# Six five-product pairs of an up projection: the work on their left forms put in program order on TensorE, ScalarE, GpSimd and VectorE

## The chip, the cores and the metric

The kernel runs on one core of one Trainium2 chip. The metric is the device time of one execution in microseconds; the core has TensorE (PE, with its weight loads PEld), VectorE (DVE), ScalarE (ACT), GpSimd (POOL) and SyncE (SP), which work side by side, each in its own order, and wait for one another on semaphores.

## The reference

One layer of a decoder over 1024 positions of width 1024: three token mixers, cross-attention, and a gated MLP. The change lies in the first matrix product of the MLP, `h @ w_up`:

```python
def conv_gated_ffn(h, w_up, conv_w, conv_b, w_down):
    u, v = jnp.split(h @ w_up, 2, axis=-1)
    u = lax.conv_general_dilated(u, conv_w[:, None, :], window_strides=(1,),
                                 padding=[(CONV_W - 1, 0)],
                                 dimension_numbers=('NWC', 'WIO', 'NWC'),
                                 feature_group_count=D_FF) + conv_b
    return (jax.nn.silu(u) * v) @ w_down
```

D_FF is 2816, so `w_up` has 5632 columns: 22 blocks of 128 for `u` and 22 for `v`.

## The kernel before, in words

**Pairs and products.** `ffn_up` goes through 22 pairs. A pair is block f of `u` and block f of `v`; their weights are the 2 x 2 blocks A11, A12, A21, A22 of a left matrix (512 rows of the contraction each), and the activations are the 2 x 2 blocks of the right one. A scheme of Strassen's kind computes the pair with seven block products in place of eight. The right forms (B11, B21, T1 to T4, B22) are made once, ahead of the loop. The left forms (A11, A12, A22 and the sums S1 to S4) are made for each pair by the generator `left` (L1292). For the first six pairs (`ne` = 6) two products, with A11 and A12, are computed earlier by `ahead` and kept in DRAM (`part`), so that these pairs have five: T2 with S2, T3 with S3, T1 with S1, T4 with A22, B22 with S4, in this order in the program. The sixteen others have seven.

**A left form.** Three steps: GpSimd makes the sum (L1308; A22 needs none), ScalarE rounds it to the high half (the cast, L1315), and the rest becomes the low half by a subtraction (L1316), on VectorE and GpSimd in turn from form to form. The form's tile `wf` has four buffers, two of each of the tags `whi` and `wlo`; a new form takes its buffer when the product that read the old one has ended.

**A product.** `prod` (L1319 to L1325): 12 matmuls of 128 x 128 by 128 x 512, that is four steps of the contraction by three combinations of halves (high-high, high-low, low-high).

**Where the products go.** T2 writes `ps_b`, one bank of PSUM. T3, T1, T4 and B22 share one tile `ps_cd` of two banks: T3 and then T4 write its first half c, T1 and then B22 its second half d. Two such tiles alternate from pair to pair. Between them VectorE reads: u2 after T2 (L1384), u3 after T3 (L1386), the upper half of vt after T1 (L1388), the lower half of vt after T4 (L1393), u after B22 (L1395). Then ScalarE's y (L1397), two y steps of VectorE (L1398, L1399), Silu on ScalarE (L1400), y times vt on VectorE (L1401); in even pairs a difference within y (L1404), in odd pairs three sums over the two pairs (L1414 to L1416, one on VectorE and two on GpSimd); DMAs of SyncE write y and the sums to DRAM, and load the next raw weights (`load`, six buffers: three pairs).

**What sets the order.** Nothing in this code writes the order out by hand. The kernel is traced in program order, and the scheduler of the framework then places each engine's instructions by priority and by when it takes their inputs to be ready, so that products of neighbouring pairs stand between one another.

Of the kernel before, what the change touches and what calls it, by code (L numbers as in the profile page):

```python
# [12 lines left out]
F32 = mybir.dt.float32  # L13
# [4 lines left out]
ALU = mybir.AluOpType  # L18
# [78 lines left out]
class K:  # L97
# [1197 lines left out]
    def left(self, r1, r2, which, sp):  # L1295

        nc = self.nc
        V, A, G = nc.vector, nc.scalar, nc.gpsimd
        q = {f"A{n}{k + 1}": r[:, 4 * k:4 * k + 4, :] for n, r in ((1, r1), (2, r2)) if r is not None for k in range(2)}
        sums = {"S1": ("A21", "A22", ALU.add), "S2": ("S1", "A11", ALU.subtract), "S3": ("A11", "A21", ALU.subtract),  # L1300
                "S4": ("A12", "S2", ALU.subtract)}

        def get(n):
            if n not in q:
                a, b, op = sums[n]
                a, b = get(a), get(b)
                q[n] = sp.tile([P, 4, P], F32, tag=n, name=n, bufs=2 if n in ("S1", "S2") else 1)
                G.tensor_tensor(out=q[n], in0=a, in1=b, op=op)  # L1308
            return q[n]

        for n in which:
            x = get(n)
            self.nform = getattr(self, "nform", 0) + 1
            f = self.wp.tile([P, 2, 4, P], F32R, tag=("whi", "wlo")[self.nform % 2], name="wf")
            A.copy(out=f[:, 0], in_=x)  # L1315
            (V if self.nform % 2 else G).tensor_tensor(out=f[:, 1], in0=x, in1=f[:, 0].bitcast(F32), op=ALU.subtract)  # L1316
            yield f

    def prod(self, ps, f, x, start, stop):  # L1319
        n = 0  # L1320
        for k in range(4):
            for a, b in ((0, 0), (0, 1), (1, 0)):
                self.nc.tensor.matmul(ps, lhsT=f[:, a, k, :], rhs=x[b][:, k, :], start=(start and n == 0), stop=(stop and n == 11),  # L1323
                                      skip_group_check=not start)
                n += 1  # L1325

    def ffn_up(self, X, act, sums, part, spill):

# [2 lines left out]
        V, A, G, T = nc.vector, nc.scalar, nc.gpsimd, nc.tensor  # L1331
        with tc.tile_pool(name="up", bufs=1) as sp:
# [4 lines left out]
            ne = part.shape[1]  # L1337

            def load(m, bufs=6):
                n = next(nraw) % bufs  # L1340
                r = self.wp.tile([P, NK, P], F32, tag="raw", name="raw") if n < 2 else \
                    self.res.tile([P, NK, P], F32, tag=f"r{n + 6 - bufs}", name="raw")
                nc.sync.dma_start(out=r, in_=I["t_up"][m])
                return r
# [84 lines left out]
            rs = [load(0), load(NFF)]  # L1429
            for f in range(NFF):  # L1430
                nx = [load(f + 1), load(NFF + f + 1)] if f + 1 < NFF else None
                pair(f, rs)
                rs = nx

# [217 lines left out]
```

## Time and profile before

| | |
|---|---|
| time, median of 3 runs | 2406.57 us (2404.03 to 2408.04) |
| the profiled execution | 2406.16 us, its span 2404.4 us |
| TensorE busy | 2308.2 us, 96% of the span |
| VectorE, ScalarE, GpSimd busy | 57%, 38%, 28% |
| mean granted clock of TensorE | 0.989 |
| first product of the five-product pairs | 1773.47 us after the span's start |

The stretch of the six pairs runs from 1773 to some 1880 us of the span; seven-product pairs follow, and from about 2170 us on the down projection, `ffn_down`. In the rows further down, times are microseconds from the start of the span; a row of the timeline gives an instruction's start, its duration, engine, source line, operation, output <- inputs, and in brackets the engine's idle time before it and what ended that. Matmuls are pipelined: in an unbroken row they follow each other by 0.23 us though each shows 0.39. "PEclk" is the granted clock as a share of the full 2.4 GHz; 0.5 is the lower level of 1.2 GHz.

### The profile page before, as it was taken

To read this page: it belongs to the slowest core of one execution; us is meant where nothing else is said; L and a number is where in the kernel's file an instruction comes from. 1 tells how busy PE (TensorE), PEld (TensorE's weight loads), DVE (VectorE), ACT (ScalarE), POOL (GpSimd) and SP (SyncE) were. 2 spreads that over 40 slices of the span, in tenths; PEclk is the share of its full clock that TensorE was granted. 3 is DMA by queue.
4 is the path that set the end of the run, shared out by engine and by line. 5 is a ranking of instruction groups with operands and counts; after the bars stand their busy time and mean duration, and the time that the engine had idled before them with its cause. 6 is when DMAs were issued, how large, how long until landed. Compare 5 with 4: busy or idle time off the path is not lost. (4 is left out here: it accounts for less than half of the span.)

```text
span 2404.4 us, 34900 instructions
## 1 busy us (share of the span) xinstructions
PE 2308.2 (96%) x13988; PEld 1883.5 (78%) x13988; DVE 1364.3 (57%) x2114; ACT 908.5 (38%) x1430; POOL 670.6 (28%) x564
## 2 busy tenths in 40 slices
PE   7999999899999999999999999999888999999998
PEld 7887768686778787887878787888766788888886
DVE  6446375747334647545464454544636666667776
ACT  6542213131223535444353223343333334335443
POOL 1011011110101333214223350142346665652001
PEclk9999999999999999999999999999999999999999
DMA  8653322221212111111103663223354232228633
GB/s 305 220 177 119 96 62 93 62 82 48 85 45 99 53 45 44 45 53 44 53 27 99 221 205 123 88 88 126 111 168 139 101 113 93 106 73 280 218 96 122
DMA packets 110930, 266.14 MB, mean 111 GB/s; under 512 B 27248, under 2 KB 31984, under 8 KB 110768
## 3 DMA queue, kind: packets, MB, share of 16 engines
q1 hardware_dynamic: 108656, 258.25, 32.2%
q0 software_dynamic: 1248, 4.46, 0.5%
q8 instruction: 110, 1.80, 0.3%
q10 hardware_dynamic: 864, 1.20, 0.1%
q14 instruction: 52, 0.43, 0.1%
HBM read 194.40 MB, written 69.47 MB: 110 GB/s over the span
## 5 line engine op out<-in xcount | busy, mean ns | idle before, releaser
L155 PE MATMUL ps_d<-hThi,whi 128*128 128x512 f32 x1056 | 426.7, 404 | 2.6 <-DVE Ktt L261 2.2
L157 PE MATMUL ps_d<-hTlo,whi 128*128 128x512 f32 x1056 | 424.9, 403 | 0.0
L159 PE MATMUL ps_d<-hThi,wlo 128*128 128x512 f32 x1056 | 424.3, 402 | 0.0
L140 ACT CAST whi<-raw 128x1024 fp32r<-128x1024 f32 (+1 forms) x170 | 166.9, 988 | 329.1 <-PE ps_d L157 153.5
L155 PEld LDWEIGHTS ps_d<-hThi,whi 128*128 128x128 f32 x1056 | 200.2, 190 | 45.5 <-issue 3.2
L143 DVE TENSOR_TENSOR wlo<-raw,whi 128x1024 fp32r<-128x1024 f32 (+1 forms) x125 | 157.6, 1268 | 137.4 <-ACT whi L140 137.4
L157 PEld LDWEIGHTS ps_d<-hTlo,whi 128*128 128x128 f32 x1056 | 200.3, 190 | 43.0 <-issue 4.6
L159 PEld LDWEIGHTS ps_d<-hThi,wlo 128*128 128x128 f32 x1056 | 200.1, 190 | 43.1 <-issue 4.2
L143 POOL TENSOR_TENSOR wlo<-raw,whi 128x1024 fp32r<-128x1024 f32 (+1 forms) x45 | 96.3, 2141 | 436.0 <-ACT whi L140 389.1
L1508 PE MATMUL ps_dn<-wd,ap 128*128 128x512 f32 x924 | 210.2, 389 | 0.0
L1508 PEld LDWEIGHTS ps_dn<-wd,ap 128*128 128x128 f32 x924 | 173.3, 188 | 36.4 <-DVE wd L1475 0.4
L1315 ACT CAST wf<-S 128x512 fp32r<-128x512 f32 x88 | 54.6, 622 | 163.3 <-PE ps_cd L1323 73.7
L1113 POOL TENSOR_SCALAR ms<-ms 128x1 f32<-128x1 f32 x30 | 11.4, 381 | 345.0 <-ACT fin L1112 159.7
L1474 ACT CAST ap<-acr 128x512 fp32r<-128x512 f32 x77 | 47.9, 622 | 105.1 <-PE ps_dn L1508 59.6
L745 DVE CUSTOM_DVE_ANT_0 a_p<-ps_s,a_bias 128x512 f32<-128x512 f32 (+3 forms) x96 | 51.7, 552 | 52.0 <-PE ps_s L743 46.8
L1316 POOL TENSOR_TENSOR wf<-S,wf 128x512 fp32r<-128x512 f32 x44 | 63.1, 1435 | 55.3 <-ACT wf L1315 55.3
L755 ACT ACTIVATE a_p<-a_p,a_nm 128x128 f32<-128x128 f32 (+7 forms) x64 | 49.1, 769 | 77.2 <-POOL a_nm L751 59.7
L159 PE MATMUL ps_d<-ohi,wlo 128*128 128x512 f32 x192 | 75.2, 392 | 2.0 <-DVE wlo L143 2.0
L1475 DVE TENSOR_TENSOR ap<-acr,ap 128x512 fp32r<-128x512 f32 x77 | 54.0, 701 | 39.7 <-ACT ap L1474 39.7
L155 PE MATMUL ps_d<-ohi,whi 128*128 128x512 f32 x192 | 75.2, 392 | 0.0
L157 PE MATMUL ps_d<-olo,whi 128*128 128x512 f32 x192 | 75.1, 391 | 0.0
L1308 POOL TENSOR_TENSOR S<-raw 128x512 f32<-128x512 f32 x44 | 58.9, 1341 | 36.7 <-DVE wf L1316 21.8
(435 smaller groups left out, 5354.6 us busy)
## 6 DMA issues: line engine op xcount, KB each, us to landing
raw<-t_in SPq DMA_DIRECT2D x66, 512.0 KB, 3.6
raw<-t_up SPq DMA_DIRECT2D x50, 512.0 KB, 3.5
th_dram<-th SPq DMA_DIRECT2D x24, 512.0 KB, 2.8
mth<-th_dram SPq DMA_DIRECT2D x24, 512.0 KB, 3.7
wdr<-ffn_w_down SPq DMA_DIRECT2D x44, 256.0 KB, 4.4
acr<-act_dram SPq DMA_DIRECT2D x44, 256.0 KB, 3.5
act_dram<-y SPq DMA_DIRECT2D x20, 512.0 KB, 2.6
acr<-sums_dram SPq DMA_DIRECT2D x33, 256.0 KB, 2.6
```

The lines of the kernel that those rows point to most:

```text
L140: nc.scalar.copy(out=hi, in_=raw)
L143: eng.tensor_tensor(out=lo, in0=raw, in1=hi.bitcast(F32), op=ALU.subtract)
L155: nc.tensor.matmul(o, lhsT=hi[:, k, :], rhs=xhi(k, h), start=(k == 0), stop=False)
L157: nc.tensor.matmul(o, lhsT=hi[:, k, :], rhs=xlo(k, h), start=False, stop=False)
L159: nc.tensor.matmul(o, lhsT=lo[:, k, :], rhs=xhi(k, h), start=False, stop=(k == nk - 1))
L745: V.tensor_tensor_reduce(out=p_[:, a:b], in0=ps[:, 0:b - a], in1=bias[:, 1024 - n + a:1024 - n + b], op0=ALU.add, op1=ALU.max, scale=1.0, ...
L755: A.activation(out=pr[c][:, 0:n], in_=pr[c][:, 0:n], func=AF.Exp, bias=nm[:, c:c + 1], accum_out=Z[:, c:c + 1])
L1308: G.tensor_tensor(out=q[n], in0=a, in1=b, op=op)
L1315: A.copy(out=f[:, 0], in_=x)
L1316: (V if self.nform % 2 else G).tensor_tensor(out=f[:, 1], in0=x, in1=f[:, 0].bitcast(F32), op=ALU.subtract)
L1475: behind("V", lambda: V.tensor_tensor(out=t[:, 1], in0=z, in1=t[:, 0].bitcast(F32), op=ALU.subtract))
L1508: T.matmul(ps[t], lhsT=a[:, p, P * t:P * t + P], rhs=w[:, q, :], start=(not onto and j == 0 and n == 0), stop=(j == NJ - 1 and n == 2), sk ...
```

## The change

A helper `inorder` and a dictionary `kinds` are added. While `kinds` is a dictionary (from pair 0 until pair 6 begins), each call chains its instruction behind the last one of the same kind, by `issue_after`, an ordering edge without a semaphore. The kinds are "T" (matmuls of a product, chained by the product's last matmul), "A" (casts on ScalarE), 0 (sums and subtractions on GpSimd) and 1 (subtractions on VectorE). VectorE's reads of PSUM, the y steps, Silu and the DMAs are not chained. Computations and their number are the same in both kernels: 11670 matmul instructions, 2116 of VectorE, 1304 of ScalarE, 569 of GpSimd, 657 of SyncE. The order differs in one stretch of each engine (487 of TensorE's positions, 82 of VectorE's, 61 of ScalarE's, 64 of GpSimd's, 43 of SyncE's).

```diff
--- before.py
+++ after.py
@@ -1305,24 +1305,36 @@
                 a, b, op = sums[n]
                 a, b = get(a), get(b)
                 q[n] = sp.tile([P, 4, P], F32, tag=n, name=n, bufs=2 if n in ("S1", "S2") else 1)
-                G.tensor_tensor(out=q[n], in0=a, in1=b, op=op)
+                self.inorder(0, lambda: G.tensor_tensor(out=q[n], in0=a, in1=b, op=op))
             return q[n]
 
         for n in which:
             x = get(n)
             self.nform = getattr(self, "nform", 0) + 1
             f = self.wp.tile([P, 2, 4, P], F32R, tag=("whi", "wlo")[self.nform % 2], name="wf")
-            A.copy(out=f[:, 0], in_=x)
-            (V if self.nform % 2 else G).tensor_tensor(out=f[:, 1], in0=x, in1=f[:, 0].bitcast(F32), op=ALU.subtract)
+            e = self.nform % 2
+            self.inorder("A", lambda: A.copy(out=f[:, 0], in_=x))
+            self.inorder(e, lambda: (G, V)[e].tensor_tensor(out=f[:, 1], in0=x, in1=f[:, 0].bitcast(F32), op=ALU.subtract))
             yield f
 
+    kinds = None
+
+    def inorder(self, n, f):
+        if self.kinds is None:
+            return f()
+        with self.tc.issue_after(self.kinds[n].ins) if n in self.kinds else ExitStack():
+            self.kinds[n] = f()
+
     def prod(self, ps, f, x, start, stop):
-        n = 0
-        for k in range(4):
-            for a, b in ((0, 0), (0, 1), (1, 0)):
-                self.nc.tensor.matmul(ps, lhsT=f[:, a, k, :], rhs=x[b][:, k, :], start=(start and n == 0), stop=(stop and n == 11),
-                                      skip_group_check=not start)
-                n += 1
+        def run():
+            n = 0
+            for k in range(4):
+                for a, b in ((0, 0), (0, 1), (1, 0)):
+                    i = self.nc.tensor.matmul(ps, lhsT=f[:, a, k, :], rhs=x[b][:, k, :], start=(start and n == 0),
+                                              stop=(stop and n == 11), skip_group_check=not start)
+                    n += 1
+            return i
+        self.inorder("T", run)
 
     def ffn_up(self, X, act, sums, part, spill):
 
@@ -1429,6 +1441,8 @@
             rs = [load(0), load(NFF)]
             for f in range(NFF):
                 nx = [load(f + 1), load(NFF + f + 1)] if f + 1 < NFF else None
+                if f in (0, ne):
+                    self.kinds = None if f else {}
                 pair(f, rs)
                 rs = nx
```

On TensorE, in the first pair, after T1 (`ps_cd_14614` belongs to the first pair, `ps_b2_14721` and `ps_cd_14722` to the second). Before:

```order
L1323 MATMUL ps_cd_14614<-T1lo_14151,wf_14655 128x512
L1323 MATMUL ps_cd_14614<-T1hi_14150,wf_14655 128x512
L1323 MATMUL ps_b2_14721<-T2hi_14141,wf_14729 128x512
L1323 MATMUL ps_b2_14721<-T2lo_14142,wf_14729 128x512
L1323 MATMUL ps_cd_14722<-T3hi_14291,wf_14747 128x512
L1323 MATMUL ps_cd_14722<-T3lo_14292,wf_14747 128x512
L1323 MATMUL ps_cd_14614<-T4hi_14159,wf_14671 128x512
```

After:

```order
L1333 MATMUL ps_cd_14614<-T1lo_14151,wf_14655 128x512
L1333 MATMUL ps_cd_14614<-T1hi_14150,wf_14655 128x512
L1333 MATMUL ps_cd_14614<-T4hi_14159,wf_14671 128x512
L1333 MATMUL ps_cd_14614<-T4lo_14160,wf_14671 128x512
L1333 MATMUL ps_cd_14614<-T4hi_14159,wf_14671 128x512 x2
```

The matmuls of the second pair's T2 and T3 that stood between T1 and T4 now stand behind B22 of the first pair.

On VectorE, from the first pair's u to the second pair's lower vt (`u2_14723`, `u3_14724`, `vt_14720` belong to the second pair, `y_14705` to the first). Before:

```order
L1384 TENSOR_TENSOR u2_14723<-ps_b2_14721,s1_14717 128x512
L1386 TENSOR_TENSOR u3_14724<-ps_cd_14722,u2_14723 128x512
L1398 SCALAR_TENSOR_TENSOR y_14705<-u_14365,par_70,y_14705 128x1024
L1399 SCALAR_TENSOR_TENSOR y_14705<-u_14365,par_70,y_14705 128x1024
L1316 TENSOR_TENSOR wf_14879<-S1_14841,wf_14879 128x512
L1388 TENSOR_TENSOR vt_14720<-ps_cd_14722,u3_14724 128x512
L1401 TENSOR_TENSOR y_14705<-y_14705,vt_14612 128x1024
L1404 TENSOR_TENSOR y_14705<-y_14705 128x512
L1393 TENSOR_TENSOR vt_14720<-ps_cd_14722,u2_14723 128x512
```

After:

```order
L1410 SCALAR_TENSOR_TENSOR y_14705<-u_14365,par_70,y_14705 128x1024
L1396 TENSOR_TENSOR u2_14723<-ps_b2_14721,s1_14717 128x512
L1411 SCALAR_TENSOR_TENSOR y_14705<-u_14365,par_70,y_14705 128x1024
L1398 TENSOR_TENSOR u3_14724<-ps_cd_14722,u2_14723 128x512
L1413 TENSOR_TENSOR y_14705<-y_14705,vt_14612 128x1024
L1416 TENSOR_TENSOR y_14705<-y_14705 128x512
L1317 TENSOR_TENSOR wf_14845<-S2_14843,wf_14845 128x512
L1400 TENSOR_TENSOR vt_14720<-ps_cd_14722,u3_14724 128x512
L1405 TENSOR_TENSOR vt_14720<-ps_cd_14722,u2_14723 128x512
```

The first pair's y steps moved ahead of the second pair's u3, and its product with vt and difference ahead of the second pair's upper vt (lines of after stand 12 further down).

## Rows read from the trace of the kernel before

**Rows 1.** Busy time by stretch: stretch, us, busy (instructions) per engine, PEclk, DMA share, GB/s.

```profile
core 0: us, PE busy (x) PEld busy (x) DVE busy (x) ACT busy (x) POOL busy (x), PEclk, DMA share, GB/s
1773.40:1800.70 27.30, 22.01 (x89) 16.89 (x88) 9.76 (x12) 6.33 (x11) 19.66 (x15) 0.94 0.43 145
1816.80:1833.30 16.50, 14.48 (x60) 10.97 (x60) 10.97 (x12) 5.29 (x7) 12.79 (x9) 1.00 0.49 175
1920.00:2170.00 250.00, 250.00 (x1098) 205.33 (x1097) 154.45 (x162) 99.81 (x145) 152.89 (x107) 1.00 0.29 103
```

**Rows 2.** Waits, 1773.4 to 1866.4: engine, line <- waited for: total us, times, longest.

```profile
ACT wf L1315 <- PE ps_cd L1323: 40.8, 18, 5.2
...
PE ps_b L1323 <- ACT wf L1315: 5.3, 5, 2.5
POOL S L1308 <- DMA raw<-t_up: 5.1, 1, 5.1
...
PE ps_cd L1323 <- ACT wf L1315: 3.1, 4, 0.9
...
PE ps_cd L1323 <- DVE u L1386: 2.2, 1, 2.2
```

**Rows 3.** Timeline of TensorE, first two pairs.

```profile
1773.47 0.40 PE L1323 MATMUL ps_cd<-T3hi,wf 128*128 128x512 f32 x1
...
1779.18 0.39 PE L1323 MATMUL ps_b<-T2hi,wf 128*128 128x512 f32 x1
...
1781.74 0.47 PE L1323 MATMUL ps_cd<-T1hi,wf 128*128 128x512 f32 x1 [2.17 <-DVE u L1386]
...
1787.16 0.50 PE L1323 MATMUL ps_b<-T2hi,wf 128*128 128x512 f32 x1 [2.45 <-ACT wf L1315]
...
1788.32 0.63 PE L1323 MATMUL ps_cd<-T4hi,wf 128*128 128x512 f32 x1
...
1792.59 0.39 PE L1323 MATMUL ps_cd<-T3hi,wf 128*128 128x512 f32 x1
...
1800.74 0.50 PE L1323 MATMUL ps_b<-T2hi,wf 128*128 128x512 f32 x1 [0.71 <-ACT wf L1315]
```

**Rows 4.** Timeline of TensorE, a steady pair's start, the stage's end, a seven-product pair.

```profile
1816.85 0.50 PE L1323 MATMUL ps_b<-T2hi,wf 128*128 128x512 f32 x1 [0.71 <-ACT wf L1315]
...
1818.21 0.50 PE L1323 MATMUL ps_b<-T2hi,wf 128*128 128x512 f32 x1 [0.63 <-POOL wf L1316]
...
1866.43 0.50 PE L1323 MATMUL ps_a<-B11hi,wf 128*128 128x512 f32 x1 [0.71 <-ACT wf L1315]
...
1906.47 0.39 PE L1323 MATMUL ps_cd<-T1hi,wf 128*128 128x512 f32 x1
...
1909.19 0.39 PE L1323 MATMUL ps_b<-T2hi,wf 128*128 128x512 f32 x1
```

**Rows 5.** Timeline of VectorE: a right form, u2, u3, y's difference, a left form's subtraction.

```profile
1775.12 0.68 DVE L1258 TENSOR_TENSOR B22lo<-ps_T,B22hi 128x512 fp32r<-128x512 f32 x1
...
1779.61 0.69 DVE L1384 TENSOR_TENSOR u<-ps_b,s 128x512 f32<-128x512 f32 x1 [3.21 <-PE ps_b L1323]
...
1780.91 0.68 DVE L1386 TENSOR_TENSOR u<-ps_cd,u 128x512 f32<-128x512 f32 x1
...
1808.71 1.67 DVE L1404 TENSOR_TENSOR y<-y 128x512 f32<-128x512 f32 x1
...
1825.56 1.78 DVE L1316 TENSOR_TENSOR wf<-S,wf 128x512 fp32r<-128x512 f32 x1
```

**Rows 6.** Timeline of ScalarE and VectorE: a pair's y steps, Silu, product with vt.

```profile
1816.91 1.24 ACT L1397 ACTIVATE y<-u,par 128x1024 f32<-128x1024 f32 x1
...
1821.39 1.05 ACT L1400 ACTIVATE y<-y 128x1024 f32<-128x1024 f32 x1
...
1819.55 1.29 DVE L1399 SCALAR_TENSOR_TENSOR y<-u,par,y 128x1024 f32<-128x1024 f32 x1
...
1840.57 1.22 DVE L1401 TENSOR_TENSOR y<-y,vt 128x1024 f32<-128x1024 f32 x1
```

## The prediction

> **What bounds the kernel now.** I read the table by stage first [rows 1]. From 1920 us on TensorE is busy for all of its stretch, so nothing that other engines gain there can count. The six five-product pairs (1773.4 to about 1880) are where it is not: 14.5 of 16.5 us in a steady pair, 22.0 of 27.3 at the start. The change touches this stage alone, and what it shifts is passed on in full, since the later stretch has no slack to give it back. Second, the list of waits of this stage [rows 2]: TensorE waits 5.3 + 3.1 us for ScalarE's casts of left forms, and once 2.2 us for u3, a read of VectorE (line 1386); the casts in turn wait mostly for products to end, which is how they get a buffer back. Third, TensorE's own order in time [rows 3, 4], for the price of a product, of a pair and of a wait.
>
> **The unit prices.** A product is 12 matmuls. A T1 of the seven-product pairs starts at 1906.47 and its follower at 1909.19 [rows 4]: 2.72 us. Five of them are 13.6 us, the floor of a pair. Four steady pairs run from 1800.74 [rows 3] to 1866.43 [rows 4]: 65.7 us for twenty products (54.4), so 11.3 us are lost, 2.8 a pair: about 0.7 for the cast of S2, 0.6 for its subtraction, 0.7 or so for the cast of S3, and 0.11 for each restart (a matmul after a wait takes 0.50 us, one in the row 0.39).
>
> The price of a hand-off through VectorE stands in the first pair [rows 3, 5]. T2's last matmul starts at 1779.18 and ends 0.39 later. VectorE starts u2 at 1779.61, does a subtraction, and ends u3 at 1780.91 + 0.68 = 1781.59; T1 starts at 1781.74. T1 writes the other half of ps_cd than u3 reads, and waited for it nevertheless. One read alone therefore costs TensorE 0.39 + 0.04 + 0.69 + 0.15, less the 0.23 at which matmuls follow each other: 1.04 us, with the restart 1.15.
>
> **What the change removes.** Products now stand T2, T3, T1, T4, B22 within a pair, and casts in the same order. The form buffers (four, two of each tag) come free in the order of use, so a cast stands three products ahead of its product instead of right before it. I take the waits for casts and subtractions as gone, 2.8 us a pair. Gone too is the cause of the longest wait, 2.45 us before T2 of the second pair [rows 3]: this T2 no longer stands among the first pair's products, so the raw tiles that GpSimd waits 5.1 us for [rows 2] are not needed until the first pair is through; SyncE also issues them before those of the fourth pair now.
>
> **What it adds.** Before, whole products of the neighbouring pairs stood between T3 and T1, ten matmuls of the next T3 between T4 and B22, and between T1 and T4 two matmuls of the next T3, whose own wait for a cast covered the read. Now T3, T1, T4 and B22 of one ps_cd follow each other directly, and each of the last three waits for the read of the one before: u3 before T1, the upper vt before T4, the lower vt before B22. That is 3 x 1.15 = 3.45 us a pair at the least, 17.05 a pair, 68.2 for four.
>
> VectorE works strictly in its own order, and two of the three reads have a queue before them. In the third and fifth pair it is u, the two y steps of the pair before with u2 between them, a left form's subtraction, then u3. From the end of B22: u 0.69, ScalarE's y 1.24 [rows 6], y 1.29, u2 0.69, y 1.29, subtraction 0.69, u3 0.69 and some 0.4 of hand-offs make 7.0 us, against 6.3 for T2, T3 and a bare hand-off: 0.7 over. In the second and fourth pair, from the start of T1, the upper vt has before it the rest of Silu (some 0.4 of 1.05), y times vt 1.22, y's difference 0.69, a subtraction 0.69, and with itself 0.69 and 0.15 it makes 3.8 us, no more than T1 and a bare hand-off.
>
> Those are VectorE's times alone. When GpSimd runs at once, operations that read two tiles of SBUF take turns with it: y's difference then took 1.67 us and a subtraction 1.78 [rows 5]. GpSimd has nine operations and 12.8 us of work in the pair shown [rows 1], and the change takes away some of what it waits for. If each queued operation meets it once, the even chain grows by some 1.0 (difference) + 0.9 (subtraction) = 1.9, and the odd one by 2.1 over the two y steps and the subtraction, 2.8 over in all, with 0.4 more before its T4. Bounds for the four pairs: 2 x (0 + 0.7) = 1.4 and 2 x (1.9 + 3.2) = 10.2. I take the upper one: GpSimd works for most of a pair, and the two alternate operation by operation. 68.2 + 10.2 = 78.4, less 65.7: **+12.7 us**.
>
> **The two ends.** With 88 matmuls of the stage issued, before stands at 1800.74, 27.3 us after 1773.47. After has the same seven products and four transposes to do, 19.4 us, then 1.5 for the first T2, which stands ahead of T3 now and waits for a B22 subtraction that VectorE did at 1775.12 [rows 5], 3.45 for the first pair's reads and 1.15 for the next u3: 25.5. **-1.8 us.** From 1866.43 to the equal point at 1909.19 before needs 42.8 for fifteen products of 40.8; the order there is nearly the old one, and of its 2.0 us of waits I leave 0.5: **-1.5 us**. Together +9.4.
>
> **The clock.** After the idle times of 2.17 and 2.45 us the granted clock fell to its lower level: T4 of the first pair takes from 1788.32 to 1792.59 [rows 3], 4.27 us against 2.72, and the stretch's mean is 0.94 [rows 1]. 1.55 us were lost. The changed order has four idle times longer than those (two of about 3.0, two of about 3.9). Bounds are 0 and 4 x 1.55 = 6.2; I take 4.8, since part of the slow matmuls runs while VectorE is late anyway. **Sum: +9.4 + 4.8 = +14.2 us.** On the profiled execution (span 2404.4 us, 2406.16 in all) that is 2420.4, on the median of the three runs, 2406.57, it is 2420.8.
>
> The rest is moved at no cost: SyncE's raw tiles have three pairs' buffers, so a load issued late by one product still has a pair of 17 us ahead of its use; ScalarE is busy for 5.3 of 16.5 us; the down projection's order is untouched. If a load did come late, it would be the 5.1 us of [rows 2] once more, under T2 to B22 of a pair.
>
> **Rivals.** (a) *The reads don't hold up the products.* T1 writes the half that u3 doesn't read. If a product waited only for reads of its own half, each read would have a whole product to hide behind, and the four pairs would fall toward their floor: 54.4 - 65.7 - 1.8 - 1.5 = -14.6; half of it, since T4 and B22 still wait for their own half behind the same queue, gives -7.3, so 2399.3. Against it: the 2.17 us [rows 3] are this very wait. Chance 0.05. The Trainium skill, PSUM — Partial Sum Buffer, section Summary: rules for kernel authors, says that PSUM may be read while a matmul runs if it targets a different bank; by that rule the wait would not be needed and the time would be that of (a). The trace disagrees for this program: it was waited for.
>
> (b) *VectorE and GpSimd seldom meet*, and the clock holds: 68.2 + 1.4 - 65.7 = +3.9, with the ends +0.6: 2407.2, no difference. It decides if GpSimd is through with a pair's sums before VectorE's queue begins. Chance 0.09, with half-way cases up to 2411.
>
> (c) *The clock stays low.* At the lower level throughout the four pairs, twenty products would cost 2.4 us more each, 48, of which the waits of 24 hide half: +24 on the sum, 2445. Against it: the steady pair is granted 1.00 with its 2.8 us of waits [rows 1], and the one fall here was over before the third pair. Chance 0.05.
>
> **How the numbers follow.** Forecast 0.81, (a) 0.05, (b) 0.09, (c) 0.05. Predicted is the forecast's 2420.8. Its own spread runs from half of the meetings and a single fall of the clock (9.4 - 4.4 + 1.2 = +6, 2412) to every fall and some 4 us more of queueing (2427); this is the range, and it leaves out (a), (c) and most of (b). About 0.2% (4.8 us) is what a measurement of this kernel can tell from no change. Slower by more: the forecast and (c), 0.86; within: (b), 0.09; faster: (a), 0.05.
>
> **What would show it.** Idle time of TensorE before T1, T4 and B22 put down to VectorE's u3 and vt, three times a pair: bare ones near 1 us, T4 of the second and fourth pair near 3, T1 of the third and fifth near 3.9; a pair of 19 to 20 us; waits for casts nearly gone; two to four falls of the granted clock; the down projection unchanged and only shifted. Wrong if those waits stay near zero (a), if all are near 1 us (b), or if GpSimd's sums, not VectorE's reads, end them.

## The result and the profile after

| | before | after |
|---|---|---|
| time, median | 2405.3 us (4 runs: the three known before and one more) | 2419.48 us (4 runs, 2417.29 to 2422.04) |
| span of the profiled execution | 2404.4 us | 2420.3 us |
| last matmul of the last early product begins | 1773.15 us | 1774.71 us |
| T2 of the ninth pair begins | 1909.19 us | 1924.74 us |

The ratio is 1.0062, with a 95% interval of 1.0043 to 1.0081, that is 14.9 us slower; the two medians differ by 14.2. Forecast were 2420.8 (range 2412 to 2427) and +14.2. Of the 15.9 us between the two spans 1.56 lie ahead of the stage, where the two programs are the same, and 0.35 behind the ninth pair. The stage itself grew from 136.0 to 150.0 us, that is by 14.0.

First TensorE's waits in the stage (engine, line <- what it waited for: us in total, times, longest). They answer to the rows of TensorE in [rows 2]:

```profile
PE ps_cd L1333 <- DVE u L1398: 10.5, 5, 3.6
PE ps_cd L1333 <- DVE vt L1400: 7.2, 4, 2.7
PE ps_cd L1333 <- DVE vt L1405: 4.4, 5, 0.9
PE ps_cd L1333 <- ACT wf L1316: 0.9, 1, 0.9
```

The waits for casts, 5.3 + 3.1 us before, are down to 0.9 here and 0.8 at the stage's end. In their place stand three reads of VectorE: u3 (L1398), the upper vt (L1400), the lower vt (L1405), 22.1 us. The timeline of TensorE, first to third pair, shows them one by one (start, us, instruction, idle time before and what ended it), against [rows 3]:

```profile
1776.36 0.50 PE L1333 MATMUL ps_b<-T2hi,wf 128*128 128x512 f32 x1 [0.73 <-DVE B22lo L1258]
1782.97 0.47 PE L1333 MATMUL ps_cd<-T1hi,wf 128*128 128x512 f32 x1 [0.88 <-DVE u L1398]
1786.83 0.47 PE L1333 MATMUL ps_cd<-T4hi,wf 128*128 128x512 f32 x1 [0.88 <-DVE vt L1400]
1790.67 0.47 PE L1333 MATMUL ps_cd<-B22hi,wf 128*128 128x512 f32 x1 [0.88 <-DVE vt L1405]
1800.31 0.47 PE L1333 MATMUL ps_cd<-T1hi,wf 128*128 128x512 f32 x1 [1.21 <-DVE u L1398]
1806.04 0.47 PE L1333 MATMUL ps_cd<-T4hi,wf 128*128 128x512 f32 x1 [2.72 <-DVE vt L1400]
1809.89 0.47 PE L1333 MATMUL ps_cd<-B22hi,wf 128*128 128x512 f32 x1 [0.88 <-DVE vt L1405]
1821.91 0.76 PE L1333 MATMUL ps_cd<-T1hi,wf 128*128 128x512 f32 x1 [3.61 <-DVE u L1398]
```

A bare wait is 0.88 us. T4 of the second pair waits 2.72 and T1 of the third 3.61; the fourth and fifth pair repeat these two, with 2.72 and 3.62. What stood before u3 in the third pair is seen on VectorE and beside it on GpSimd:

```profile
1814.90 2.35 DVE L1410 SCALAR_TENSOR_TENSOR y<-u,par,y 128x1024 f32<-128x1024 f32 x1 [1.31 <-ACT y L1409]
1817.17 0.68 DVE L1396 TENSOR_TENSOR u<-ps_b,s 128x512 f32<-128x512 f32 x1
1817.78 1.71 DVE L1411 SCALAR_TENSOR_TENSOR y<-u,par,y 128x1024 f32<-128x1024 f32 x1
1819.41 1.75 DVE L1317 TENSOR_TENSOR wf<-S,wf 128x512 fp32r<-128x512 f32 x1
1821.08 0.68 DVE L1398 TENSOR_TENSOR u<-ps_cd,u 128x512 f32<-128x512 f32 x1
...
1813.64 1.28 POOL L1317 TENSOR_TENSOR wf<-raw,wf 128x512 fp32r<-128x512 f32 x1 [6.90 <-ACT wf L1316]
1814.88 1.29 POOL L1308 TENSOR_TENSOR S<-raw,S 128x512 f32<-128x512 f32 x1
1816.13 2.28 POOL L1308 TENSOR_TENSOR S<-raw 128x512 f32<-128x512 f32 x1
1818.48 2.13 POOL L1308 TENSOR_TENSOR S<-S,raw 128x512 f32<-128x512 f32 x1
```

GpSimd stood still for 6.90 us, behind a subtraction whose cast was not done, and then makes three sums in a row, just while VectorE does the two y steps and a subtraction. These take 2.35, 1.71 and 1.75 us, against 1.28 to 1.29 for a y step [rows 6] and 0.69 for a subtraction alone. u2 and u3, which read one operand from PSUM, take 0.68 as ever. T4 of the second pair is late in the same way: of what stands before its upper vt, y's difference and a subtraction run while GpSimd makes two sums, and take 1.67 and 1.54 us in place of 0.69 each:

```profile
1801.95 1.67 DVE L1416 TENSOR_TENSOR y<-y 128x512 f32<-128x512 f32 x1
...
1803.75 1.54 DVE L1317 TENSOR_TENSOR wf<-S,wf 128x512 fp32r<-128x512 f32 x1
```

The granted clock, by stretches of the third, fourth and fifth pair (stretch, us, busy time and instructions by engine, PEclk):

```profile
1821.30:1827.90 6.60, 5.46 (x12) 3.80 (x12) 4.54 (x4) 0.42 (x1) 5.93 (x4) 0.50 0.41 163
1848.60:1851.80 3.20, 3.20 (x9) 2.12 (x7) 0.00 (x0) 0.00 (x0) 0.00 (x0) 0.50 0.00 0
1865.70:1868.90 3.20, 3.20 (x9) 2.46 (x8) 2.36 (x2) 0.28 (x1) 3.20 (x2) 0.50 0.40 164
```

In each of the three stretches it is at the lower level, 1.2 GHz. The first stretch takes in the end of a long wait, the 3.61 us; the other two begin 1.1 and 0.8 us after the end of one. The fourth long wait, before T4 of the second pair, has no such stretch behind it.

### The profile page after: what moved, and what is told of

Read it like the earlier page. It is cut to its first block, busy times and chain, and to the rows that moved or that the text cites. A ratio compares the mean times of both kernels' runs of the same rounds, so it can differ in the third digit from the quotient of the medians.

```text
span 2420.3 us, 34925 instructions
## 1 busy us (share of the span) xinstructions
PE 2313.6 (96%) x13988; PEld 1888.8 (78%) x13988; DVE 1367.0 (56%) x2114; ACT 909.7 (38%) x1430; POOL 672.5 (28%) x564
## 5 line engine op out<-in xcount | busy, mean ns | idle before, releaser
L1333 PE MATMUL ps_cd<-T1hi,wf 128*128 128x512 f32 x176 | 61.6, 412 | 10.5 <-DVE u L1398 10.5
```

What stands on the lines that cost most here:

```text
L1333: i = self.nc.tensor.matmul(ps, lhsT=f[:, a, k, :], rhs=x[b][:, k, :], start=(start and n == 0), stop=(stop and n == 11), skip_group_check ...
```

## Experiments

The part ahead of the stage, which no experiment is about, differs by more than 5 us from one profile to another (the stage begins between 1769.3 and 1774.7 us). So beside the ratio of the times stands the length of the stage in the profiled execution, from the start of the last early product's last matmul to the first T2 matmul of the thirteenth pair: 213.0 us before, 227.3 after. The kernel before was timed anew with each group of runs (medians from 2402.9 to 2405.7 us), and each ratio is to the kernel before of its own group.

| | median, us | ratio to before (95%) | stage, us | against before |
|---|---|---|---|---|
| the change | 2419.5 | 1.0062 (1.0043 to 1.0081) | 227.3 | +14.3 |
| products chained alone | 2406.9 | 1.0012 (1.0001 to 1.0022) | 215.0 | +2.0 |
| forms chained alone | 2412.7 | 1.0037 (1.0025 to 1.0049) | 219.5 | +6.5 |
| change without sums | 2407.3 | 1.0022 (1.0006 to 1.0037) | 215.8 | +2.8 |
| change, subtractions on VectorE | 2414.0 | 1.0049 (1.0034 to 1.0064) | 222.8 | +9.8 |
| change with two tiles | 2393.6 | 0.9950 (0.9935 to 0.9965) | 199.6 | -13.4 |
| two tiles, products chained | 2388.5 | 0.9945 (0.9930 to 0.9960) | 198.2 | -14.9 |
| two tiles alone | 2388.1 | 0.9934 (0.9911 to 0.9957) | 197.3 | -15.7 |
| half a pair apart | 2396.9 | 0.9971 (0.9960 to 0.9982) | 204.9 | -8.1 |
| half a pair apart, products chained | 2402.0 | 0.9996 (0.9986 to 1.0005) | 208.7 | -4.3 |

**Two tiles.** My theory was that the reads hold TensorE up because c and d are one tile.

```diff
-                cd = self.dps.tile([P, 1024], F32, tag="d", name="ps_cd")
-                c, d = cd[:, 0:512], cd[:, 512:1024]
+                if f < ne:
+                    c, d = (self.dps.tile([P, 1024], F32, tag="d", name=t)[:, 0:512] for t in ("ps_c", "ps_d2"))
+                else:
...
```

> The changed kernel, but in the six five-product pairs T3 and T4 write a PSUM tile of their own (c) and T1 and B22 another (d), one bank each, in place of two halves of one two-bank tile; the order of the products is the changed one. Theory (the reads hold up TensorE because the halves c and d are one tile, so that a product waits for a read of the half that it does not write): each read then has a product of 2.72 us or more to hide behind, the idle times of 0.88 us before T1, T4 and B22 go, those of 2.72 and 3.61 us shrink below 1 us, the granted clock has no fall in the stage, and the time drops by 10 to 18 us against the changed kernel, to 2401 to 2410, that is at or below the kernel before. Rival (VectorE's queue is late by itself, whatever the tile): T1 and T4 still wait 2 us or more in every second pair, the drop is under 6 us, 2414 or more.

No PSUM is added: the pool has two buffers of two banks each, and c and d now take one buffer each and use its first bank. Every pair thus uses both buffers, and neighbouring pairs no longer alternate between them. TensorE's order is the changed one in the first five pairs. The gain was larger than expected: the expectation had set the time at that of the kernel before, though a stage without these waits has to fall below it by the waits for casts as well. TensorE's waits in the stage:

```profile
PE ps_c L1333 <- DVE u L1401: 1.9, 2, 0.9
PE ps_d L1333 <- ACT wf L1316: 1.2, 1, 1.2
PE ps_d L1333 <- DVE vt L1403: 0.9, 1, 0.9
```

22.1 us of waits for reads became 2.8. VectorE's y steps stay as slow as in the changed kernel (1.8 us in the mean), and in the third pair the same steps stand in the same order before u3; that costs nothing once a product stands between. Before the upper vt of the second pair VectorE has one subtraction less here. So the tile is shown to be the cause of the waits, and VectorE's lateness alone is not enough.

**One part of the change at a time.** In `inorder`, all kinds but "T" are passed through unchained; the second kernel has `n == "T"` in the same place:

```diff
-        if self.kinds is None:
+        if self.kinds is None or n != "T":
             return f()
```

> Only one part of the change: the products are chained in program order, the casts, sums and subtractions are left to the scheduler. TensorE's order is then that of the changed kernel word for word. Theory (the order of the products alone makes the loss): within 3 us of the changed kernel, 2416 to 2423. Rival (the chains on ScalarE, GpSimd and VectorE put the subtractions ahead of the reads and make the long waits of 2.72 and 3.61 us): only the bare waits are left, 2410 or less.

> The other part alone: casts, sums and subtractions are chained in program order, the products are left to the scheduler, which puts T2 and T3 of the next pair between the products of a pair again. Theory (the order of the products makes the loss, and the order of the forms takes waits for casts away): no idle time of TensorE for u3 and vt, 2395 to 2406. Rival (the chains of the forms cost): slower than the kernel before by 4 us or more, 2410 and up.

Both went the rival's way. With the products chained alone, TensorE's order is that of the changed kernel, and yet only 2.0 us of the stage's 14.3 are left. TensorE's timeline, third pair:

```profile
1815.06 0.47 PE L1333 MATMUL ps_cd<-T1hi,wf 128*128 128x512 f32 x1 [1.03 <-DVE u L1398]
1819.26 0.47 PE L1333 MATMUL ps_cd<-T4hi,wf 128*128 128x512 f32 x1 [1.20 <-DVE vt L1400]
1823.10 0.47 PE L1333 MATMUL ps_cd<-B22hi,wf 128*128 128x512 f32 x1 [0.88 <-DVE vt L1405]
```

The three waits are there, nearly bare, and no fall of the clock. VectorE and GpSimd ahead of that T1:

```profile
1810.63 1.29 DVE L1410 SCALAR_TENSOR_TENSOR y<-u,par,y 128x1024 f32<-128x1024 f32 x1 [1.31 <-ACT y L1409]
...
1812.44 0.68 DVE L1317 TENSOR_TENSOR wf<-S,wf 128x512 fp32r<-128x512 f32 x1
1813.04 1.28 DVE L1411 SCALAR_TENSOR_TENSOR y<-u,par,y 128x1024 f32<-128x1024 f32 x1
...
1809.37 1.30 POOL L1317 TENSOR_TENSOR wf<-raw,wf 128x512 fp32r<-128x512 f32 x1 [0.46 <-ACT wf L1316]
1813.20 2.25 POOL L1308 TENSOR_TENSOR S<-raw,S 128x512 f32<-128x512 f32 x1 [2.53 <-DVE wf L1317]
```

The same steps are in VectorE's queue, the subtraction ahead of the second y step instead of behind it, but GpSimd has little to do beside them: it stands still during the first two, and its one sum begins 0.16 us after the second y step and is itself the one that takes longer. The steps take 1.29 + 0.68 + 1.28 us in place of 2.35 + 1.71 + 1.75. The difference, 2.56 us, is nearly the difference of the two waits, 3.61 and 1.03. Over the whole stage TensorE waits 15.5 us for the three reads in place of 22.1; these 6.6 us and the 5.6 that the three falls of the clock cost come to 12.2, of the 12.3 by which the two stages differ. Which of the chains does it can be told from the order of the instructions alone (the next two kernels were not timed): products and GpSimd chained give the same order on TensorE, ScalarE, VectorE and GpSimd as all four kinds, products and ScalarE give VectorE's order as with products alone. It is GpSimd's chain, with what the scheduler then does on VectorE: in the second and fourth pair it also puts a subtraction behind y's product with vt, which stands ahead of that product when the products alone are chained.

With the forms chained alone the products are placed by the scheduler, but in another order than before: T1 follows B22 of the pair before. Its u, u2 and u3 then stand in a row, 0.69 us each, and T1 waits 2.3 to 3.1 us for the last of them. T2 of the second pair also waits 3.83 us for a cast, and the clock falls twice. The row of a wait for u3:

```profile
1798.73 0.39 PE L1333 MATMUL ps_cd<-B22hi,wf 128*128 128x512 f32 x1
1801.45 0.47 PE L1333 MATMUL ps_cd<-T1hi,wf 128*128 128x512 f32 x1 [2.33 <-DVE u L1398]
...
1799.16 0.69 DVE L1407 TENSOR_TENSOR u<-ps_cd,u 128x512 f32<-128x512 f32 x1 [1.37 <-PE ps_cd L1333]
1799.89 0.69 DVE L1396 TENSOR_TENSOR u<-ps_b,s 128x512 f32<-128x512 f32 x1
1800.61 0.69 DVE L1398 TENSOR_TENSOR u<-ps_cd,u 128x512 f32<-128x512 f32 x1
```

**GpSimd's sums.** In `left`, while `kinds` is a dictionary, a sum is not made:

```diff
                 a, b = get(a), get(b)
+                if self.kinds is not None:
+                    q[n] = a
+                    return a
```

> The changed kernel with GpSimd's sums of left forms left out in the six pairs (a form is made from the first of the two blocks, so the numbers that come out are others); casts, subtractions, products and their chains stay. Measured so far: with the products alone chained the time is 2406.9 and TensorE waits 1.0 to 1.6 us where the changed kernel waits 2.72 and 3.61. Theory (the long waits come from GpSimd's sums, which in strict order come in a row beside VectorE's y steps and slow them: 2.35 and 1.71 us in place of 1.29): without the sums the y steps take 1.3 us, T4 and T1 wait 1.6 us at most, no fall of the granted clock in the stage, 2403 to 2409. Rival (VectorE's or ScalarE's strict order makes them, whatever GpSimd does): the waits of 2.7 and 3.6 us stay and the time is above 2414.

The time is as the theory had it. T4 of the second pair waits 1.61 us and that of the fourth 0.88 (2.72 both in the changed kernel), T1 of the third and fifth 1.03 (3.61 and 3.62), and the clock has no fall. One wait of 2.17 us, before T4 of the fifth pair, was not expected. Sums are made again at that point, those of the seventh pair, and beside them VectorE's product with vt takes 2.07 us and its sum 1.65. Nor did all y steps go back to 1.3 us: the second one still takes 1.72 in the mean. This run does not hold VectorE's order fixed, since the scheduler puts some subtractions earlier once the sums are gone. The next run gives the sums back and takes GpSimd's waits for casts away:

```diff
-            e = self.nform % 2
+            e = 1 if self.kinds is not None else self.nform % 2
```

> The changed kernel with all subtractions of left forms of the six pairs on VectorE, five a pair in place of two or three; GpSimd keeps the sums alone, in the same strict order, with no step among them that waits for a cast. Theory (in the changed kernel GpSimd stands behind a subtraction that waits for a cast, which waits for a buffer that a product holds, and so it makes the sums late and in a row, beside the y steps): GpSimd's wait for casts of 37.3 us goes, its sums are made earlier in the pair, T4 and T1 wait under 2 us, and the time is 2403 to 2411 although VectorE has 1.7 us more to do in a pair. Rival (the number of steps in VectorE's queue is what counts): two more subtractions stand before u3 and vt, the waits get longer by 0.7 us or more, 2419 and up.

Neither came true. GpSimd's wait for casts went, but now it waits 45.9 us for sums' tiles that VectorE's subtractions hold, and makes the sums in a row later in the pair, beside VectorE's product with vt and its sum. First VectorE, then GpSimd, then the T4 that they make late:

```profile
1816.54 2.31 DVE L1413 TENSOR_TENSOR y<-y,vt 128x1024 f32<-128x1024 f32 x1
1818.88 1.64 DVE L1426 TENSOR_TENSOR asum<-y 128x512 f32<-128x512 f32 x1
1820.44 0.68 DVE L1400 TENSOR_TENSOR vt<-ps_cd,u 128x512 f32<-128x512 f32 x1
...
1816.03 1.73 POOL L1308 TENSOR_TENSOR S<-raw 128x512 f32<-128x512 f32 x1
1817.84 2.13 POOL L1308 TENSOR_TENSOR S<-S,raw 128x512 f32<-128x512 f32 x1
...
1821.27 0.47 PE L1333 MATMUL ps_cd<-T4hi,wf 128*128 128x512 f32 x1 [2.62 <-DVE vt L1400]
```

The y steps are back at 1.28 us and T1 at 1.03 to 1.08; T4 waits 2.6 to 2.76 in three pairs, each with a fall of the clock behind it. The sums were moved, and the long wait moved with them. That ties the wait to the sums more closely than their removal does.

**Two tiles without the change.**

> Two one-bank tiles c and d as in the run with 2393.6, but with the products alone chained, so that GpSimd's sums are placed by the scheduler. The two causes were measured apart: tile (12 us below the kernel before) and the chain of GpSimd (12.6 us between 2419.5 and 2406.9). Theory (with two tiles each read has a product to hide behind, so that GpSimd's order has hardly anything left to cost): within 3 us of 2393.6, 2390 to 2396. Rival (both gains add up): 2386 or less.

> The kernel before with nothing of the change, but with two one-bank tiles c and d in the six five-product pairs. Theory (the order of the products is worth something only where the reads don't hold up TensorE; it takes the waits for casts away, some 2.8 us a pair before): without the chain the scheduler still puts products of the next pair between those of a pair, waits for casts stay, and the time lies between the kernel before and the two kernels with two tiles and chained products (ratios 0.995 and 0.9945 to before): 0.997 to 1.000. Rival (the two tiles alone give it all): 0.9955 or less.

The time of the first, 2388.5 us, lies between the two ranges given for it, but its kernel before was 2.9 us faster than that of the run with 2393.6; by the ratios the theory held, and the gains don't add up. The second went the rival's way. With the tiles apart, GpSimd's chain costs little: 1.5 us of the stage, and the two ratios, 0.9950 and 0.9945, overlap. That the chain of the products would still be worth something was not borne out. Two tiles alone, with 2388.1, are as fast as anything here (the intervals of the two kernels with 0.9934 and 0.9945 overlap), and a steady pair of theirs is at the floor of the prediction, 13.6 us, with TensorE busy throughout:

```profile
1809.99:1823.59 13.60, 13.60 (x62) 11.27 (x60) 11.40 (x12) 5.22 (x7) 12.27 (x8) 1.00 0.63 226
1823.59:1837.19 13.60, 13.60 (x62) 11.27 (x60) 12.45 (x13) 5.36 (x7) 12.22 (x8) 1.00 0.26 96
```

The scheduler's order is another one there: T1, two matmuls of the next T2, T4, the rest of T2, B22, the next T3. So this run shows what the tiles bring together with the order that follows from them.

**Half a pair apart.** T4 and B22 of a pair are traced between the products of the next, with one tile as before and a second buffer for u2. `pair` becomes a generator that stops before T1, T4 and B22; `g` is the pair f, `prev` the pair before:

```diff
+                    next(g)
+                    if f:
+                        next(prev)
+                    next(g)
+                    if f:
+                        list(prev)
```

> The same chains as in the changed kernel, one PSUM tile ps_cd of two banks as before, but the program of two neighbouring five-product pairs is written half a pair apart: T2 and T3 of a pair, then T4 of the pair before, T1 of the pair, then B22 of the pair before. u2 gets a second buffer, since two pairs are under way at once. So each read of PSUM has a product of the other tile to hide behind. Theory (what costs is that the products of one tile follow each other directly, not that casts and sums stand in the order of the products): idle times before T1, T4 and B22 under 0.5 us, waits for casts as short as in the changed kernel, a steady pair of 13.6 to 14.5 us, and 2390 to 2400 in all, below both kernels. Rival (the strict order of casts, sums and subtractions is itself a cost, by waits of ScalarE for GpSimd and of VectorE's subtractions): waits for left forms show up on TensorE and the time stays above 2405.

> The program half a pair apart as in the run with 2396.9 and one tile ps_cd, but with the products alone chained. Theory: as with two tiles, every read has a product to hide behind, so that the order of the forms changes little, 2391 to 2398. Rival (the order of the forms costs here as well): 5 us or more away from 2396.9.

The first time was as expected, though steady pairs take 13.6 to 16.3 us; the second went the rival's way. A product of the other pair hides most of a read, so both kernels are faster than the change. T1 still waits 0.9 to 2.74 us for u3, where the wait is long behind two y steps (2.27 and 2.28 us in the second of these runs, with GpSimd at work). Here it is the kernel with the products alone chained that is slower, by 4 us of the stage: GpSimd waits 21.1 us for raw weights there, since the scheduler puts sums of a later pair first, and at the stage's start T2 of the second pair waits 2.21 and 2.75 us for its form; the clock falls twice. Strict order of the forms is thus not bad in itself.

## Why the prediction was right

**The unit prices held.** From T1 to T4 of the first pair are 3.86 us, one product of 2.72 and a hand-off of 1.14; predicted were 1.15.

**The ends.** From the place behind the last early product (1775.03; 1773.47 in [rows 3]) to T1 of the second pair are 25.3 us in place of 27.3 (predicted 25.5), at the end 40.7 in place of 42.8. Together -4.1 us; predicted were -3.3. The first T2 did wait for B22's subtraction, and the wait of T2 in the second pair was gone.

**The four pairs.** From T1 of the second pair, 1800.31, to T1 of the sixth, 1884.06, are 83.75 us against 65.7. The prediction had 78.4 and 4.8 for the clock, 83.2. T4 of the second and fourth pair lie 1.84 us over the bare wait (predicted 1.9), T1 of the third and fifth 2.73 (predicted 2.8). Of the 0.4 more before T4 of those pairs nothing was seen, while T1 of the second and fourth wait 0.3 longer than bare.

**The clock.** Three falls, not four: T1 of the third pair takes 2.47 us longer than a bare step, T4 of the fourth and T1 of the fifth 1.6 each, 5.6 in all; predicted were 4.8, as four falls of 1.2. The 2.72 us before T4 of the second pair brought no fall. So the clock cost 0.8 us more than put down and the ends gave 0.8 more back: that the sum of +14.2 came within 0.2 of the stage's +14.0 is luck in part.

**The step that was right in size and not in its reason** is that VectorE meets GpSimd. I took the upper bound since GpSimd "works for most of a pair". It does, but that does not decide it. Over the four pairs GpSimd's share is the same before and after, first before, then after (stretch, us, busy time and instructions by engine, PEclk):

```profile
1800.74:1866.43 65.69, 57.95 (x241) 43.99 (x241) 45.28 (x48) 22.61 (x29) 44.33 (x31) 1.00 0.42 138
1800.31:1884.06 83.75, 63.87 (x242) 48.11 (x243) 51.54 (x47) 22.18 (x30) 56.37 (x36) 0.92 0.32 110
```

These are 44.33 of 65.69 us and 56.37 of 83.75, 67% in both, and before a y step takes 1.28 us. With the products alone chained the share is 64% (45.20 of 70.40 us in four pairs), and the waits are nearly bare. In the changed kernel GpSimd waits 36.6 us for casts in the stage, 11.9 before, and then makes its sums in a row, which is why the steps queued ahead of u3 and vt meet them. In kernels where GpSimd is busier, as with two tiles, the y steps are as slow, and nobody waits for them. It is the strict order on GpSimd, and not its load, that put the sums there.

**The rivals.** (b), that VectorE and GpSimd seldom meet, gave 2407.2; with the products alone chained they meet less where a product waits, T1 and T4 wait 0.88 to 1.58 us, and the time is 2406.9. So the bare waits are about worth the casts that they replace, and the loss is the queue and the clock behind it. (a) was false for one tile of two banks and comes true as soon as there are two tiles, and by more than the 2399.3 that were put down for it: 2393.6 us in the changed order and 2388.1 in the scheduler's. The halving of the gain was wrong there: T4 and B22 do wait for their own half, but only 2.8 us in the whole stage in the changed order. In the scheduler's order u3 is read from 1808.54 on beside T1, whose matmuls keep their distance of 0.23 us:

```profile
1807.04 0.39 PE L1323 MATMUL ps_c<-T3hi,wf 128*128 128x512 f32 x1
1807.27 0.39 PE L1323 MATMUL ps_d<-T1hi,wf 128*128 128x512 f32 x1
...
1809.54 0.39 PE L1323 MATMUL ps_d<-T1lo,wf 128*128 128x512 f32 x1
1809.76 0.39 PE L1323 MATMUL ps_d<-T1hi,wf 128*128 128x512 f32 x1
...
1808.54 0.68 DVE L1389 TENSOR_TENSOR u<-ps_c,u 128x512 f32<-128x512 f32 x1
```

The Trainium skill, PSUM — Partial Sum Buffer, section Summary: rules for kernel authors, allows just this, a read of another bank while a matmul runs. The trace agrees once the program names the banks apart; with one tile the program itself asked for the wait.

(c), a clock that stays low, did not come: it was back after each fall.

## What to carry to other kernels

Give each PSUM accumulator that is read by itself a tile of its own: here that was worth 0.66%, 16 us, and took no more of PSUM. Ordering the work around one tile of two banks cost 2 to 14 us of the stage where the products of a pair followed each other directly, and at its best, half a pair apart with all chains, gained 8 us. Before chaining an engine into program order, ask what its first waiting instruction holds back, and beside whose work that will then run; here GpSimd had no more sums to make, but made them later and in a row. A long queue costs only where a product waits behind it, so look at the wait and not at the duration.

## What was not expected of the hardware

The turns that VectorE and GpSimd take showed more clearly than expected. The two y steps, grouped by line in the stage of after (count, busy us, mean ns, idle time before):

```profile
L1411 DVE SCALAR_TENSOR_TENSOR y<-u,par,y 128x1024 f32<-128x1024 f32 x4 | 7.5, 1870 | 0.0
L1410 DVE SCALAR_TENSOR_TENSOR y<-u,par,y 128x1024 f32<-128x1024 f32 x4 | 7.3, 1818 | 4.0 <-ACT y L1409 4.0
```

Before, and with the subtractions all on VectorE, the same groups have 1.28 us in the mean, so the surcharge is 0.5 to 0.6 us a step in the mean, while reads with one operand in PSUM stay at 0.68 to 0.69 in every timeline shown. The Trainium skill, SBUF — State Buffer, section Who interferes with whom, states that a VectorE instruction with two inputs in SBUF contends with a GpSimd instruction that reads SBUF, and one with at most one SBUF input, outside the two-port modes, does not; the rows agree.

Which of the two is held up shows as well: it is the one that begins second. In the changed kernel the y step of 1814.90 begins 0.02 us after a sum and takes 2.35 us, the sum 1.29. With the products alone chained the sum of 1813.20 begins 0.16 us after a y step and takes 2.25 us, the y step 1.28. Over all eleven traces a step of VectorE with both inputs in SBUF and an operation of GpSimd begin within 0.3 us of each other some 70 times in the stage. The earlier one then keeps its own time to within 0.2 us, and the later one takes 0.3 to 1.2 us longer. So what a sum costs VectorE hangs on which of the two is first, be it by 0.02 us.
